# Attention with forget gates: the gates' sums ride in the second score product, under the low halves of the keys

## The chip, the cores and the metric

The kernel runs on one core of a Trainium2 chip. The metric is the device time of one execution in microseconds. Three runs of the kernel before took 1725.48, 1726.19 and 1727.21 us; the median is 1726.19 us.

## The reference

Two transformer blocks on 512 tokens. The change lies in the second block, in its eight attention heads with forget gates ("forget heads" below, `fox` in the code):

```python
def _fox_attention(q, k, v, log_f):
    """softmax(q.k/sqrt(d) + c[t] - c[s]) over s <= t, c = cumsum(log f)."""
    scale = HEAD_DIM ** -0.5            # HEAD_DIM = 64, 8 heads
    c = jnp.cumsum(log_f.astype(jnp.float32), axis=-1)
...
        logits = jnp.einsum('bhqd,bhkd->bhqk', qi, k, preferred_element_type=jnp.float32) * scale
        logits = logits + ci[..., None] - c[:, :, None, :]
        logits = jnp.where(kpos[None, :] <= qpos[:, None], logits, -jnp.inf)
        p = jax.nn.softmax(logits, axis=-1)
        return jnp.einsum('bhqk,bhkd->bhqd', p.astype(v.dtype), v)
```

The term `c[t]` is the same for all keys of a query and drops out of the softmax. What the kernel needs is `-q.k*scale + c[s]`, the score with its sign turned, and the kernel's softmax works on that.

## The kernel before

Everything lies transposed in SBUF: 128 partitions (features) by 512 tokens. float32 accuracy comes from splitting: each operand `x` is kept as a high part `xh` (rounded to the matmul's format, fp32r) and a low part `xl = x - xh`; `hi_lo` and `pair` (L120 to L150) do this, the high part by a cast on ScalarE (L136), the low part by a subtraction on VectorE (L140). A linear layer takes three matmuls for each block of 128 features (`mm3`, L208 to L210): high by high, high by low, low by high. These three lines are the bulk of the kernel. Weights are loaded by SP in pieces of 128 by 1024 into a ring of three raw tiles `wr` (`wload`, L180), then split into `wh` and `wl`.

A forget head has only 64 features, half of the 128 rows that TensorE reduces over, and the kernel fills both halves. `place` (L850) copies 64 rows of one tile into the upper or lower half of another, by a DMA of 128 KB on SP's queue. For a head, `stacked` makes one tile `stk` with the queries' high part above and their low part below; `doubled` makes two tiles `dbl`: the keys' high part twice, and the keys' low part twice. One matmul of the first pair then gives `qh.kh + ql.kh`, one of the second `qh.kl + ql.kl`. That takes six copies a head. `fox_inputs` (L1286) does it for a pair of heads; from pair 1 on it first computes the pair's queries and keys with two linear layers.

The gates' sums `c` come from a small matmul over the normed input (16 matmuls of 40 by 512, L1177), then on VectorE and ScalarE an addition, a scale, a bias, log-sigmoid (`Abs`, `Exp`, `Ln`), and a cumulative scan (L1189). They are kept in `cf`, whose other rows are zero: the high part of head `hd` in row `hd` (L1192, ScalarE), the low part in row `32 + hd` (L1193, VectorE).

`fox_scores` (L1263) runs over four blocks of 128 queries. Block `i` sees `w = 128, 256, 384 or 512` keys and has three matmuls into one PSUM bank: the two above (L1269, L1270) and a third (L1271), in which column `hd` of the constant `sel_r` picks rows `hd` and `32 + hd` of `cf` and adds their sum to every query's row. Then `softmax`: VectorE reads the bank, adds the mask and finds the minimum (L814), ScalarE takes the exponential with its sum (L171), VectorE the reciprocal (L817), ScalarE scales (L821). The scores use three banks in turn (`AT`, banks 70, 71, 72). `fox_values` transposes the weights of the attention on TensorE (L828), splits them, and multiplies by the values (L1210, L1211).

Between the heads stand independent products: the queries and keys of later heads and of the next kind of head (`sb_raw`), and `memory` (L945), which loads four `mem` tiles, squares them for a norm on ScalarE (L349), and splits them (`mh` on ScalarE, L138; `ml` on VectorE, L142).

The order of instructions on each engine is not that of the code. The tile framework's scheduler sets it (`TileContext(schedule_with_timeline_sim=True)`, L1694), from its own costs; at run time every engine, and SP's queue of DMAs, then runs in that order. SBUF tiles come from a list of 84 slots, given out in the order in which they were freed (`A`, `free`).

Of the kernel before, what the change touches and what calls it, by code (L numbers as in the profile page):

```python
# [11 lines left out]
F32R = mybir.dt.float32r  # L12
# [5 lines left out]
P = 128  # L18
T = 512
# [19 lines left out]
for _n, _w in _VECS:  # L39
# [4 lines left out]

_CONSTS = [
    ("ident", 128), ("later", 128), ("incl", 128), ("strict", 128), ("nstrict", 128),
    ("ones", 128), ("chunk", 14), ("sel", 8), ("invf", 1), ("sgn", 1),
    ("mchunk", 512), ("mcausal", 512),
]
COFF = {}  # L50
# [8 lines left out]
def two_blocks(ctx: ExitStack, tc: tile.TileContext, d, dbg=None):  # L59
    nc = tc.nc  # L60
    V, S, G, PE = nc.vector, nc.scalar, nc.gpsimd, nc.tensor
# [14 lines left out]
    def A(name, dt=F32, cols=T):  # L76
        if cols > 256 or len(spare_half) < 3:
            i = spare.popleft()
            low[0] = min(low[0], len(spare))
            ap = ar.tile([P, T], dt, tag="slot%d" % i, name=name)[:, :cols]  # L80
            owner[id(ap)] = (spare, i, ap, name)
        else:
            i = spare_half.popleft()
            ap = ar.tile([P, 256], dt, tag="half%d" % i, name=name)[:, :cols]
            owner[id(ap)] = (spare_half, i, ap, name)
        return ap

    def free(*xs):
        for x in xs:
            if isinstance(x, (tuple, list)):  # L90
                free(*x)
            else:
                home, i = owner.pop(id(x))[:2]
                home.append(i)
# [118 lines left out]
    def lin(w, n, hs, cols=T, k0=0, after=None):  # L213

        kt = len(hs)
        ps = MM()
        wt = wtile(w, n, kt, k0)
        for k in range(kt):
            r = mm3(ps[:, :cols], wpart(wt, k), hs[k], k == 0, k == kt - 1)
            if k == 0 and after:  # L220
                order(r, after)
        free(wt[1])
        return ps
# [202 lines left out]
    def C(name):  # L426
        i = COFF[name]
        return con[:, i:i + dict(_CONSTS)[name]]
# [9 lines left out]
    def const_r(name):  # L438
        c = C(name)
        o = cst.tile([P, c.shape[1]], F32R, name=name + "_r")  # L440
        V.tensor_copy(o, c)
        return o

    later_r, incl_r, ones_r = const_r("later"), const_r("incl"), const_r("ones")
    ident_r, nstrict_r, sel_r = const_r("ident"), const_r("nstrict"), const_r("sel")
    chunk_r = const_r("chunk")

    def normed(src_tiles, gain, n, before=None, **kw):
# [11 lines left out]
    def evac(ps, name, Rt, scale=None, cols=T):  # L460
        o = A(name)
        if scale is None:
            V.tensor_tensor(o[:, :cols], ps[:, :cols], Rt[:, :cols], ALU.mult)
        else:
            V.scalar_tensor_tensor(o[:, :cols], ps[:, :cols], scale, Rt[:, :cols], ALU.mult, ALU.mult)
        return o
# [76 lines left out]
    def chained(src, gain, n, step=None):  # L543

        hs = [(A("hh", F32R), A("hl", F32R)) for _ in src]
        st = Stat(n, esq=S, eadd=G)
        for c in HALVES:
            steps, los = [], []
            for k, x in enumerate(src):
                steps.append(step(k, c) if step else [])  # L550
                hold[:] = hi_lo(hs[k][0][:, c], hs[k][1][:, c], x[:, c], vcol(gain, k))
                los.append(hold[1])
                st.add(x[:, c], c)
            if step:

                line = []
                for k in range(KD + 2):
                    line += steps[k] if k < KD else []
                    line += [los[k - 2]] if k > 1 else []
                for later, earlier in zip(line[1:], line):  # L560
                    order(later, earlier)
        return hs, st
# [60 lines left out]
    hs, pss, wps, marks = [], [MM(), MM()], [], []  # L623
    for k, x in enumerate(xs):
        hs.append(pair("h", x, vcol("pre_mix", k)))
        marks.append(list(made))
        if k in (0, 2, 4):
            c = PARTS[k // 2]
# [11 lines left out]
    R, rt = st.done()  # L640
# [13 lines left out]
    for t in range(NT):  # L654
        q = slice(t * P, (t + 1) * P)
        ps = AT()
# [153 lines left out]
    def softmax(ps, w, mask):  # L810

        s, p = A("sc", F32, w), A("p", F32, w)
        mn, su = small(1), small(1)
        V.tensor_tensor_reduce(s[:, :w], ps[:, :w], mask, 1.0, BIG, ALU.add, ALU.min, mn)  # L814
        act(table_exp[0], p[:, :w], s[:, :w], AF.Exp, bias=mn, scale=-1.0, accum_out=su)
        free(s)
        V.reciprocal(su, su)  # L817
        if table_exp[0] == "exp_tanh":
            V.tensor_scalar(p[:, :w], p[:, :w], su, None, ALU.mult)
        else:  # L820
            S.activation(p[:, :w], p[:, :w], AF.Copy, scale=su)  # L821
        return p
# [25 lines left out]
    def place(o, rows, src, a):  # L848

        nc.sync.dma_start(f(o[rows]), f(src[a]))  # L850

    HALF = (slice(0, 64), slice(64, 128))

    def stacked(p, hh):

        o = A("stk", F32R)
        for rows, src in zip(HALF, p):
            place(o, rows, src, HALF[hh])
        return o
# [104 lines left out]
    for n in range(KD):  # L964
        g = gbs[n]
        ps = lin(d["w_o_mla"], n, oms)
# [6 lines left out]
    def post_norm(fs, st, gain, xs):  # L973

        def step(k, c):
            r = V.scalar_tensor_tensor(fs[k][:, c], fs[k][:, c], vcol(gain, k), st.R[:, c], ALU.mult, ALU.mult)  # L976
            q = (G if k % 2 else V).tensor_tensor(xs[k][:, c], xs[k][:, c], fs[k][:, c], ALU.add)
            if c.stop == T:
                free(fs[k])
                if k == KD - 1:  # L980
                    free(st.R)
            return [r.ins] if k % 2 else [r.ins, q.ins]
        return step
# [23 lines left out]
    hs, sth = chained(xs, "pre_ffn", DM, post_norm(fs, st, "post_mix", xs))  # L1007
# [12 lines left out]
    R = sth.R  # L1020
# [57 lines left out]
    for n in range(G1, KF, 2):  # L1078
# [4 lines left out]
        else:  # L1083
            for j, g in enumerate(zg):
                act("silu", g, g, AF.Silu)
                ps = lin(d["w_fgu"], 2 * (n + j) + 1, ns)
                V.tensor_tensor(g, g, ps, ALU.mult)
                hid.append(repair(g))
        if n + 2 == G2:
            for m in range(KD):  # L1090
                ps = lin(d["w_fd"], m, hid, k0=G1)
# [24 lines left out]
    hs, sth = chained(xs, "attn_norm", DM, post_norm(fs, st, "post_ffn", xs))  # L1116
# [45 lines left out]
    R = sth.R  # L1162
# [11 lines left out]
    ps = MM()  # L1174
    for k in range(KD):
        for part in range(2):
            PE.matmul(ps[0:40], lhsT=wfr[:, 40 * k:40 * k + 40], rhs=hs[k][part],  # L1177
                      start=k + part == 0, stop=k + part == KD)
# [11 lines left out]
    cf = A("cf", F32R)  # L1190
# [2 lines left out]
    V.tensor_tensor(cf[32:40], ef[0:8], f(cf[0:8]), ALU.subtract)  # L1193
    free(zf, ef)

    def doubled(p, hh):

        out = []
        for src in p:
            o = A("dbl", F32R)  # L1200
            for rows in HALF:
                place(o, rows, src, HALF[hh])
            out.append(o)
        return out
# [55 lines left out]
        free(ah, al)  # L1260
        return r

    def fox_scores(hd, qst, k2):  # L1263
        pt = []
        for i in range(NT):
            w = (i + 1) * P
            q = slice(i * P, (i + 1) * P)
            ps = AT()
            PE.matmul(ps[:, :w], lhsT=qst[:, q], rhs=k2[0][:, :w], start=True, stop=False)  # L1269
            PE.matmul(ps[:, :w], lhsT=qst[:, q], rhs=k2[1][:, :w], start=False, stop=False)  # L1270
            PE.matmul(ps[:, :w], lhsT=sel_r[:, hd:hd + 1].broadcast_to([P, P]), rhs=cf[:, :w],  # L1271
                      start=False, stop=True)
            pt.append(softmax(ps, w, C("mcausal")[:, T - w:]))
        free(qst, k2)
        return pt

    def fox_values(hd, pt, o):
# [8 lines left out]
    def fox_inputs(hp):  # L1286
        if hp:
            xq = evac(lin(d["w2T"], hp, hs), "fq", R, -0.125)
            xk = evac(lin(d["w2T"], 4 + hp, hs), "fk", R)
        else:  # L1290
            xq, xk = firsts[0], firsts[4]
        pq, pk = repair(xq), repair(xk)
        out = [(stacked(pq, hh), doubled(pk, hh)) for hh in range(2)]
        free(pq, pk)
        return out

# [33 lines left out]
    for hd in range(8):  # L1330
# [12 lines left out]
        else:  # L1343
            sraw.append(sb_raw(hd // 2))
        last = (hd, pt, o)
    free(hs, R)
    share(mm=(0, 1, 2), at=(3, 4, 5, 6), op=(7,))
    sin_ = [sb_inputs(*sraw[0])]
    fox_values(*last)
# [62 lines left out]
    hs, sth = chained(xs, "xattn", DM)  # L1412
# [8 lines left out]
    R = sth.R  # L1421
# [45 lines left out]
    q1 = [repair(q, eh=G) for q in firstq[4:]]  # L1467
# [19 lines left out]
    hs, sth = chained(xs, "ffn_norm", DM)  # L1487
# [5 lines left out]
    R = sth.R  # L1493
# [115 lines left out]
def _constants():  # L1609
    i = np.arange(P)  # L1610
    a, b = i[:, None], i[None, :]
    c = {}
    c["ident"] = a == b
    c["later"] = (a // 64 == b // 64) & (a > b)
    c["incl"] = a >= b
    c["strict"] = b > a
    c["nstrict"] = np.where(b > a, 0.0, -BIG)
    c["ones"] = np.ones((P, P))
    c["chunk"] = a // 64 + 6 == np.arange(14)[None, :]
    c["sel"] = (a < 64) & (a % 32 == np.arange(8)[None, :])  # L1620
    c["invf"] = np.array(_INVF, np.float32)[i % 32][:, None]
    c["sgn"] = np.where(a % 64 < 32, -1.0, 1.0)
    z = np.zeros((P, T - P))
    c["mchunk"] = np.concatenate([z, np.where(b // 64 <= a // 64, 0.0, BIG)], 1)
    c["mcausal"] = np.concatenate([z, np.where(b <= a, 0.0, BIG)], 1)
    return np.concatenate([np.asarray(c[n], np.float32) for n, _ in _CONSTS], 1)
# [72 lines left out]
```

## Time and profile before

| what | value |
|---|---|
| median of three runs | 1726.19 us |
| the profiled execution | 1726.83 us |
| its span, first to last instruction | 1725.1 us |
| TensorE busy, 930 to 1060 us (scores of the forget heads) | 128.69 of 130 us |
| third products (L1271) | 32, from 955.7 to 1057.6 us |

The profile is of one execution. In its rows a matmul's duration overlaps the next one's; how far apart two starts are says what a matmul costs while TensorE is never idle. "Idle before" in a row is the time in which an engine waited, with the instruction that ended the wait. DMA rows of SP show when a transfer was issued; "to landing" is from there to the end of the transfer.

### The profile page before, as it was taken

The numbers are of one execution on the slowest core, as the hardware profiler recorded it, in microseconds if no ns is written. First come the engines' busy times: TensorE is split into PE (matmuls) and PEld (weight loads), VectorE is DVE, ScalarE is ACT, GpSimd is POOL, SyncE is SP. The second block draws the span as 40 slices with busy tenths as digits, with TensorE's granted clock in tenths as the row PEclk, the third lists the DMA queues.
The fourth block names the chain that finished last, engine by engine and source line by source line (L and its number), as shares of the span: only waits on it lengthen the run. The fifth ranks groups of instructions, "written<-read, shape, count | busy, mean of one in ns | idle before, by whom it ended". The sixth has DMA issues, their size and how long they took to land.

```text
span 1725.1 us, 25847 instructions
## 1 busy us (share of the span) xinstructions
PE 1700.7 (99%) x9706; PEld 1485.8 (86%) x9706; DVE 1197.4 (69%) x2390; ACT 886.9 (51%) x1821; POOL 92.0 (5%) x109
## 2 busy tenths in 40 slices
PE   9999999999999999999999999999999999999998
PEld 7888888888888889989998888898898988988987
DVE  7547764677666767747777656877866598865863
ACT  6534454555454444424445656778535454552553
POOL 1000001000004000000013000000200200000000
PEclk9999999999999999999999999999999999999999
DMA  6212152223540322332333353442314123232321
GB/s 228 86 49 74 63 171 86 79 80 97 193 168 1 108 86 77 123 110 74 124 110 100 97 134 102 131 135 83 126 51 133 50 71 106 95 120 74 108 88 50
DMA packets 63951, 174.30 MB, mean 101 GB/s; under 512 B 8081, under 2 KB 13393, under 8 KB 63825
## 3 DMA queue, kind: packets, MB, share of 16 engines
q1 hardware_dynamic: 63408, 172.44, 32.3%
q8 instruction: 76, 1.25, 0.3%
q14 instruction: 51, 0.41, 0.1%
q10 hardware_dynamic: 288, 0.14, 0.0%
q0 software_dynamic: 128, 0.07, 0.0%
HBM read 153.74 MB, written 4.19 MB: 92 GB/s over the span
## 4 chain that ended last, share of the span: by engine, by line
PE 88%; DVE 4%; DMA 3%; ACT 2%; issue 1%; POOL 0%; POOLq 0%; DVEq 0%; SPq 0%; ACTq 0%
PE bank L208 27%; PE bank L210 27%; PE bank L209 27%; DVE wl L140 1%; PE bank L828 1%; PE bank L1251 1%; ACT wh L136 1%; DVE f L976 1%; DMA wr<-w_mq 0%; DMA wr<-w1K 0%; PE bank L1211 0%; DVE hl L142 0%; PE bank L1210 0%; DMA wr<-w1T 0%; PE bank L376 0%
## 5 line engine op out<-in xcount | busy, mean ns | idle before, releaser
L136 ACT CAST wh<-wr 128x512 fp32r<-128x512 f32 (+2 forms) x534 | 311.7, 606 | 356.9 <-PE bank L209 129.8
L140 DVE TENSOR_TENSOR wl<-wr,wh 128x512 fp32r<-128x512 f32 (+1 forms) x534 | 349.4, 671 | 162.4 <-ACT wh L136 137.7
L210 PE MATMUL bank<-hh,wl 128*128 128x512 f32 (+1 forms) x868 | 305.1, 353 | 0.8 <-DVE wl L140 0.8
L208 PE MATMUL bank<-hh,wh 128*128 128x512 f32 (+1 forms) x868 | 303.4, 355 | 2.2 <-DVE z L1016 1.7
L209 PE MATMUL bank<-hl,wh 128*128 128x512 f32 (+1 forms) x868 | 304.6, 352 | 0.7 <-DVE hl L142 0.6
L209 PE MATMUL bank<-prl,wh 128*128 128x256 f32 (+1 forms) x760 | 253.5, 334 | 0.0
L210 PE MATMUL bank<-prh,wl 128*128 128x256 f32 (+1 forms) x760 | 253.0, 334 | 0.0
L208 PE MATMUL bank<-prh,wh 128*128 128x256 f32 (+1 forms) x760 | 250.9, 334 | 0.2 <-ACT wh L136 0.2
L210 PEld LDWEIGHTS bank<-hh,wl 128*128 128x128 f32 x868 | 164.3, 189 | 23.0 <-DVE wl L140 2.1
L208 PEld LDWEIGHTS bank<-hh,wh 128*128 128x128 f32 x868 | 163.3, 190 | 23.7 <-ACT hh L138 3.4
L209 PEld LDWEIGHTS bank<-hl,wh 128*128 128x128 f32 x868 | 164.4, 189 | 22.0 <-DVE hl L142 2.0
L208 PEld LDWEIGHTS bank<-prh,wh 128*128 128x128 f32 x760 | 144.3, 190 | 14.1 <-ACT wh L136 0.4
L209 PEld LDWEIGHTS bank<-prl,wh 128*128 128x128 f32 x760 | 144.4, 190 | 13.8
L210 PEld LDWEIGHTS bank<-prh,wl 128*128 128x128 f32 x760 | 144.3, 190 | 13.8
L209 PE MATMUL bank<-nl,wh 128*128 128x512 f32 (+1 forms) x440 | 148.4, 337 | 0.0
L208 PE MATMUL bank<-nh,wh 128*128 128x512 f32 (+1 forms) x440 | 148.3, 337 | 0.0
L210 PE MATMUL bank<-nh,wl 128*128 128x512 f32 (+1 forms) x440 | 147.9, 337 | 0.0
L209 PEld LDWEIGHTS bank<-nl,wh 128*128 128x128 f32 x440 | 83.5, 190 | 8.9
L210 PEld LDWEIGHTS bank<-nh,wl 128*128 128x128 f32 x440 | 83.5, 190 | 8.9
L208 PEld LDWEIGHTS bank<-nh,wh 128*128 128x128 f32 x440 | 83.5, 190 | 8.8
L333 POOL TENSOR_TENSOR rtok<-sm,minus_half 128x2 f32<-128x2 f32 (+1 forms) x20 | 17.2, 859 | 1194.1 <-DVE sm L332 1194.1
L136 ACT CAST wh<-s 128x512 fp32r<-128x512 f32 x72 | 43.9, 620 | 65.0 <-DVE s L297 37.9
(400 smaller groups left out, 3354.4 us busy)
## 6 DMA issues: line engine op xcount, KB each, us to landing
wr<-w_up SPq DMA_DIRECT2D x38, 512.0 KB, 3.5
wr<-w_fgu SPq DMA_DIRECT2D x32, 512.0 KB, 3.6
wr<-w1T SPq DMA_DIRECT2D x16, 512.0 KB, 3.5
wr<-w_gate SPq DMA_DIRECT2D x16, 512.0 KB, 4.3
wr<-w_fd SPq DMA_DIRECT2D x16, 512.0 KB, 4.0
wr<-w2T SPq DMA_DIRECT2D x16, 512.0 KB, 4.0
wr<-w_dn SPq DMA_DIRECT2D x16, 512.0 KB, 3.5
wr<-w1K SPq DMA_DIRECT2D x12, 512.0 KB, 4.2
```

The costliest lines, as they stand in the source:

```text
L136: r = S.copy(hi, src) if eh is S else V.tensor_copy(hi, src)
L140: q = el.tensor_tensor(lo, src, f(hi), ALU.subtract)
L208: r = PE.matmul(ps, lhsT=ah, rhs=bh, start=first, stop=False)
L209: PE.matmul(ps, lhsT=ah, rhs=bl, start=False, stop=False)
L210: PE.matmul(ps, lhsT=al, rhs=bh, start=False, stop=last)
L333: G.tensor_tensor(y, v, minus_half[:, :y.shape[1]], ALU.pow)
L828: PE.transpose(tp[:, i * P:(i + 1) * P], ps_tiles[i][:, b * P:(b + 1) * P], C("ident"))
L976: r = V.scalar_tensor_tensor(fs[k][:, c], fs[k][:, c], vcol(gain, k), st.R[:, c], ALU.mult, ALU.mult)
L1251: PE.matmul(z[:, (b2 - b) * P:w], lhsT=lt, rhs=part[:, :T - b2 * P], start=False, stop=False)
```

## The change

The third product of a score goes. Its two rows of sums enter by the second product. Head `hd` now has four tiles: `qst` (queries' high part above the low part, as before), `k0` (keys' high part twice, as before), `q1` (queries' high part above, the lower half of `pick` below), and `k1` (keys' low part above, 64 rows of `cf` from row `hd` below, so that the head's sums lie in rows 64 and 96). `pick` is a new tile of 512 equal columns, one in rows 64 and 96 and zero elsewhere. The second matmul gives `qh.kl + c`; the product `ql.kl` is no longer computed. A head takes eight copies in place of six, two of them from `pick` and `cf`.

```diff
-    ("ones", 128), ("chunk", 14), ("sel", 8), ("invf", 1), ("sgn", 1),
+    ("ones", 128), ("chunk", 14), ("sel", 1), ("invf", 1), ("sgn", 1),
...
-    ident_r, nstrict_r, sel_r = const_r("ident"), const_r("nstrict"), const_r("sel")
+    ident_r, nstrict_r = const_r("ident"), const_r("nstrict")
...
+    pick = A("pick", F32R)
+    V.tensor_copy(pick, C("sel").broadcast_to([P, T]))
...
-    def fox_scores(hd, qst, k2):
+    def fox_scores(hd, qst, q1, k0, k1):
...
-            PE.matmul(ps[:, :w], lhsT=qst[:, q], rhs=k2[0][:, :w], start=True, stop=False)
-            PE.matmul(ps[:, :w], lhsT=qst[:, q], rhs=k2[1][:, :w], start=False, stop=False)
-            PE.matmul(ps[:, :w], lhsT=sel_r[:, hd:hd + 1].broadcast_to([P, P]), rhs=cf[:, :w],
-                      start=False, stop=True)
+            PE.matmul(ps[:, :w], lhsT=qst[:, q], rhs=k0[:, :w], start=True, stop=False)
+            PE.matmul(ps[:, :w], lhsT=q1[:, q], rhs=k1[:, :w], start=False, stop=True)
             pt.append(softmax(ps, w, C("mcausal")[:, T - w:]))
-        free(qst, k2)
+        free(qst, q1, k0, k1)
...
-        out = [(stacked(pq, hh), doubled(pk, hh)) for hh in range(2)]
+        out = []
+        for hh in range(2):
+
+            k0, q1, k1 = A("dbl", F32R), A("stk", F32R), A("dbl", F32R)
+            hd, h = 2 * hp + hh, HALF[hh]
+            qst = stacked(pq, hh)
+            for rows in HALF:
+                place(k0, rows, pk[0], h)
+            place(q1, HALF[0], pq[0], h)
+            place(q1, HALF[1], pick, HALF[1])
+            place(k1, HALF[0], pk[1], h)
+            place(k1, HALF[1], cf, slice(hd, hd + 64))
+            out.append((qst, q1, k0, k1))
...
-    free(hs, R)
+    free(hs, R, pick)
...
-    c["sel"] = (a < 64) & (a % 32 == np.arange(8)[None, :])
+    c["sel"] = (a == 64) | (a == 96)
```

The scheduler then sets another order. Three places show it. In the new file the two products of a score are L1272 and L1273.

The first place is VectorE in the norm ahead of the forget heads, where `f`, `x`, `sq` and `hl` are steps of that norm and `wfr` holds the gates' weights. Before:

```order
L1031 TENSOR_TENSOR f<-f,bank_69 128x256
L1171 TENSOR_SCALAR wfr<-con 128x320
L977 TENSOR_TENSOR x<-x,f 128x256
L976 SCALAR_TENSOR_TENSOR f<-f,vec,R 128x256 x2
L362 TENSOR_TENSOR sq<-sq 128x256
L1172 CAST wfr<-wf 128x8x8
```

Now, on the same engine at the same place:

```order
L1031 TENSOR_TENSOR f<-f,bank_69 128x256
L1171 TENSOR_SCALAR wfr<-con 128x320
L977 TENSOR_TENSOR x<-x,f 128x256
L976 SCALAR_TENSOR_TENSOR f<-f,vec,R 128x256 x2
L1197 CAST pick<-con 128x512
L362 TENSOR_TENSOR sq<-sq 128x256
L1172 CAST wfr<-wf 128x8x8
```

The cast that makes `pick` was put among the steps of the norm.

The second place is TensorE where head 0's first three scores get their last product; banks 66 and 69 collect products of linear layers. Before:

```order
L208 MATMUL bank_66<-hh,wh 128x512
L1271 MATMUL bank_70<-cf,sel_r 128x128
L1271 MATMUL bank_71<-cf,sel_r 128x256
L1271 MATMUL bank_72<-cf,sel_r 128x384
L209 MATMUL bank_66<-hl,wh 128x512
```

Now:

```order
L210 MATMUL bank_69<-hh,wl 128x512
L1273 MATMUL bank_70<-dbl,stk 128x128
L1273 MATMUL bank_71<-dbl,stk 128x256
L1273 MATMUL bank_72<-dbl,stk 128x384
L1272 MATMUL bank_70<-dbl,stk 128x512
L1273 MATMUL bank_70<-dbl,stk 128x512
L1272 MATMUL bank_72<-dbl,stk 128x256
L1273 MATMUL bank_72<-dbl,stk 128x256
L210 MATMUL bank_66<-hh,wl 128x512
```

The last product comes eight linear products earlier, and the next two scores, which before stood 14 linear products later, follow at once.

The third place is SP's queue and ScalarE just behind the sums. SP before, from the last weight load ahead of pair 1's copies on (`wr` of `w2T` are weights of coming linear layers):

```order
L180 DMA wr_75<-w2T 128x1024
L180 DMA wr_76<-w2T 128x1024
L850 DMA dbl<-prh 64x512 x2
L850 DMA dbl<-prl 64x512 x2
L850 DMA dbl<-prh 64x512 x2
L850 DMA dbl<-prl 64x512 x2
L180 DMA wr_74<-w2T 128x1024
```

SP now:

```order
L180 DMA wr_75<-w2T 128x1024
L850 DMA dbl<-prh 64x512 x3
L850 DMA dbl<-prl 64x512
L850 DMA dbl<-cf 64x512 x3
L850 DMA dbl<-prh 64x512
L850 DMA dbl<-prl 64x512
L850 DMA dbl<-cf 64x512
L950 DMA mem<-memT 128x512
L180 DMA wr_76<-w2T 128x1024
L180 DMA wr_74<-w2T 128x1024
```

ScalarE now, a little later (`p` and `sc` are the softmax's tiles):

```order
L349 ACTIVATE sq<-mem 128x256
L138 ACTIVATE mh<-mem,vec 128x256
L349 ACTIVATE sq<-mem 128x256
L138 ACTIVATE mh<-mem,vec 128x256
L171 ACTIVATE p,sm_101<-sc,sm_100 128x512
L821 ACTIVATE p<-p,sm_97 128x256
L171 ACTIVATE p,sm_106<-sc,sm_105 128x256
L136 CAST wh<-wr_76 128x512
```

The last `mem` load and a weight load that stood ahead of the sums on SP stand behind four copies of them, and on ScalarE the passes over that `mem` tile stand ahead of softmax pieces and of the cast of that weight.

## The prediction

> **What bounds the kernel now.** The first view is the page: busy time of each engine, and the chain that ended last.
>
> ```profile
> PE 1700.7 (99%) x9706; PEld 1485.8 (86%) x9706; DVE 1197.4 (69%) x2390; ACT 886.9 (51%) x1821; POOL 92.0 (5%) x109
> PE 88%; DVE 4%; DMA 3%; ACT 2%; issue 1%; POOL 0%; POOLq 0%; DVEq 0%; SPq 0%; ACTq 0%
> ```
>
> TensorE holds 88% of the chain. The second view is by stretches (busy time of PE, PEld, DVE, ACT, POOL, then the granted clock): 930 to 1060 us holds the forget heads' scores, 1060 to 1330 us the stage after them.
>
> ```profile
> 930.00:1060.00 130.00, 128.69 (x645) 106.11 (x644) 82.47 (x212) 81.78 (x198) 0.69 (x1) 1.00 0.43 112
> 1060.00:1330.00 270.00, 264.25 (x1666) 236.23 (x1665) 205.32 (x432) 171.25 (x388) 16.33 (x20) 1.00 0.38 111
> ```
>
> TensorE idles 130 - 128.69 = 1.3 us in the stage that is changed, and the clock is full. So a matmul that goes saves what it spaces out in the issue order, and a new wait of TensorE costs its whole length: there is nothing that it could hide in.
>
> **What is removed.** The third view is TensorE's timeline at the removed matmuls (start, duration, operation).
>
> ```profile
> 943.47 0.40 PE L209 MATMUL bank<-hl,wh 128*128 128x512 f32 x1
> ...
> 955.49 0.39 PE L208 MATMUL bank<-hh,wh 128*128 128x512 f32 x1
> 955.72 0.57 PE L1271 MATMUL bank<-cf,sel_r 128*128 128x128 f32 x3
> 956.12 0.40 PE L209 MATMUL bank<-hl,wh 128*128 128x512 f32 x1
> ...
> 959.78 0.40 PE L1271 MATMUL bank<-cf,sel_r 128*128 128x512 f32 x1
> 960.02 0.28 PE L1269 MATMUL bank<-dbl,stk 128*128 128x256 f32 x1
> ```
>
> Durations overlap, so I take starts. Three third products, of 128, 256 and 384 columns, hold TensorE from 955.72 to 956.12, 0.40 us; the one of 512 from 959.78 to 960.02, 0.24 us. That is 0.64 us a head; 8 heads give **5.1 us**. The first two products stay, with other operands in the same shapes.
>
> The Trainium skill ("TensorE: Matmul & The Clock Gate", Back-to-back issue gap) states a spacing of N/2.4 ns plus 2.5 ns for warm matmuls. By it a head's four would be 543 ns and the eight heads 4.3 us, an estimate from that page, and the whole change 0.8 us worse. The rows are longer at 512 columns (0.24 us where it gives 0.216) and for the three together (0.40 against 0.327), so the trace's 5.1 us stands.
>
> **What is added.** A head needs eight half-tile copies on SP's queue instead of six, 16 more in all.
>
> ```profile
> 935.07 1.11 SPq L850 DMA_DIRECT2D stk<-prh  x2
> 936.28 1.19 SPq L850 DMA_DIRECT2D stk<-prl  x2
> ```
> ```profile
> DMA to landing us min/median/max: 2.2/2.4/2.9
> ```
>
> Two copies take 1.2 us of SP, 0.6 us each, and land 2.4 us after issue (the second fence is of the `dbl` copies). 16 x 0.6 = 9.6 us, of 130 us in which SP mostly waits. I cost that at nothing where copies run ahead, with TensorE's long blocks of other products as cover; without that cover every late microsecond shows.
>
> VectorE makes `pick`, and the order puts this in the norm ahead of the stage, where TensorE waits at the end of a chain through VectorE and GpSimd:
>
> ```profile
> 907.97 0.43 PE L384 MATMUL bank<-con,rtok 128*128 128x128 f32 x2 [0.99 <-POOL rtok L333]
> ```
> ```profile
> L136 DVE CAST prh<-mq 128x512 fp32r<-128x512 f32 x6 | 2.6, 425 | 0.2
> ```
>
> No row shows a cast from one broadcast column. The nearest is the plain 512-column cast, 0.43 us; the passes of 0.69 us below are the far end, and nothing is the near end, if another step of the chain is late. I take **0.5 us** more of that wait.
>
> **What is moved: when the gates' sums are needed.** Before, the sums `cf` entered last, by a matmul that read them directly. Now they are finished, then copied by DMA, before the second product.
>
> ```profile
> 938.03 0.40 PE L208 MATMUL bank<-hh,wh 128*128 128x512 f32 x1
> ```
> ```profile
> 938.43 3.71 PE bank L1177 x16
> ```
> ```profile
> 948.21 0.69 DVE L463 TENSOR_TENSOR fk<-bank,R 128x512 f32<-128x512 f32 x1 [0.29 <-PE bank L210]
> ...
> 951.24 0.68 DVE L1193 TENSOR_TENSOR cf<-ef,cf 8x512 fp32r<-8x512 f32 x1
> ```
>
> `cf` is ready at 951.92 and its first reader starts at 955.72: 3.8 us of slack. In the new order the 16 gate matmuls stand two rows later (0.46 us), but the product of `fk`, which VectorE evacuates ahead of the scan, ends 0.4 us earlier; I get the same 952.0. The first copy of `cf` goes out at 952.05 and lands at **954.5** (954.3 to 955.0). TensorE comes to the second products earlier now: from 938.03, 3 products, the gate matmuls, 3 products, 0.40 us of first scores, then 44 products of 0.227 us (53 spacings from 943.47 to 955.49): 938.03 + 0.69 + 3.72 + 0.68 + 0.40 + 9.98 = **953.5**. So a new wait of 1.0 us (0.8 to 1.5); behind it stand products whose operands are ready, and they wait too.
>
> Right behind, TensorE waits for VectorE to empty the score banks, since the 14 products that filled that time stand elsewhere now.
>
> ```profile
> 955.98 0.29 DVE L814 CUSTOM_DVE_ANT_0 sc<-bank,con 128x128 f32<-128x128 f32 x1 [1.26 <-PE bank L1271]
> ...
> 957.01 0.08 DVE L814 DVE_READ_ACCUMULATOR2_ANT sm<- 128x1 f32 x1
> ```
>
> VectorE starts 0.26 us after the first score and needs 1.1 us for three (955.98 to 957.09). Two scores that reuse these banks stand in that time, then a product whose low weights VectorE makes only after it: about 0.85 us of waits.
>
> **The next late thing** is ScalarE. The last `mem` load now stands behind four copies of `cf` on SP, and four ScalarE passes over it stand ahead of a softmax piece, then of the cast of a weight.
>
> ```profile
> L349 ACT ACTIVATE sq<-mem x8: 400/408/426, 923.4 to 950.6; 128x256 f32<-128x256 f32 x8
> L138 ACT ACTIVATE mh<-mem,vec x8: 493/496/507, 923.7 to 957.2; 128x256 fp32r<-128x256 f32 x8
> ...
> DMA to landing us min/median/max: 2.6/3.4/4.0
> ```
> ```profile
> 960.95 0.72 ACT L171 ACTIVATE p<-sc,sm 128x512 f32<-128x512 f32 x1 [1.46 <-DVE sm L814]
> 961.58 0.19 ACT L171 ACTIVATION_READ_ACCUMULATOR p<-sc,sm 128x1 f32 x1
> 961.67 0.49 ACT L171 ACTIVATE p<-sc,sm 128x256 f32<-128x256 f32 x1
> 962.08 0.19 ACT L171 ACTIVATION_READ_ACCUMULATOR p<-sc,sm 128x1 f32 x1
> 962.17 1.10 ACT L821 ACTIVATE p<-p,sm 128x512 f32<-128x512 f32 x2
> ...
> 966.20 0.62 ACT L136 CAST wh<-wr 128x512 fp32r<-128x512 f32 x1 [0.17 <-PE bank L1211]
> ```
>
> Six copies behind 952.05 put the load at 955.75; it lands at 959.15 (958.4 to 959.8). Four passes (1.8 us, 1.45 as they overlap by 0.1 each), the exponentials of 512 and 256 columns (0.72 and 0.50 by their starts), a scaling (0.4) and the cast (0.62) end at **962.9** (962.1 to 963.5). TensorE's own work from 953.5 to that weight's product is 22 products of 0.227, the scores and small ones, 6.4 us: 959.9. So the three waits together are 3.0 us, fixed by this last; the two earlier alone give 1.85.
>
> In exchange two waits of before in this stretch can go.
>
> ```profile
> PE bank L1269 <- DVE sm L814: 0.4, 1, 0.4
> PE bank L376 <- DVE sm L814: 0.4, 1, 0.4
> ```
>
> With TensorE's restart they are 0.45 us apiece, 0.9 us. Given back: 3.0 - 0.9 = 2.1 us, or 1.0 if the load is early. I take 1.9, near the median landings.
>
> **The sum.** 5.1 - 0.5 - 1.9 = 2.7 us less. From the profiled execution's 1726.83 (span 1725.1 and 1.7 around it) that is 1724.1; it lies 0.64 above the median 1726.19, so on the median **1723.5**, 0.16% less. The orders differ on to 1330 us, which I can't cost row by row: the 5.75 us of idle there bound a gain; I take nothing, and 1.5 us either way.
>
> **Rivals.**
>
> *The whole gain arrives.* `cf`'s copy or the `mem` load comes early, and the two old waits go: 5.1 less, 1721.1 (1719.6 to 1722). For it: 3.8 us of slack today. Against: 952.0 plus 2.4 is later than 953.5 by any row.
>
> *The gain is eaten.* Loads at their late ends (4.0 and 2.9 us) add 1 us, the later heads or the next stage 2: about 1726, no change. For it: SP carries added copies and weights in one line. Against: from head 2 on a score comes well after its copies.
>
> *Slower: SP starves TensorE of weights.* The four `cf` copies wait for VectorE, and the next four weight loads stand behind them on SP. Each microsecond that `cf` is later than 952.0 delays these loads, casts and products one for one. It decides against the change once the extra waits pass 5.1 + 3.5 = 8.6 us, so with `cf` 6 us late or a second such block at heads 4 to 7: 1730 and more. Against: `cf`'s chain has fixed steps. The Trainium skill ("TensorE: Matmul & The Clock Gate", Part 1: The HAM clock gate) says that an idle window of about 3.4 us halves TensorE's clock, which would add to such a block; no row here shows it.
>
> That the third product doesn't really go is excluded by the order: no row of it is left.
>
> **How the numbers follow.** About 0.2% (3.5 us) is what a measurement can tell from no change, so the border is 1722.7, inside the forecast's own spread (1721.8 to 1725.3). Forecast 0.52, whole gain 0.24, eaten 0.16, slower 0.08. Faster: 0.24 and a quarter of the forecast, 0.37; slower 0.08; same 0.55. Range: the whole gain with 1.5 us of luck after it, 1719.6; the eaten case and 1.3 more, 1727.3. Beyond lie the slower case and thin tails.
>
> **What would show it.** Right: no third product; a wait for a `dbl` copy near 953.5 of 1 us, one for a cast of ScalarE near 962 with `mem` ahead of it; the wait for `rtok` near 908 at 1.5 us; idle time from 930 to 1060 of 3.2 us instead of 1.3. Wrong: no wait at the first second product (`cf` or its copy was earlier), or over 2 us at a later head's score or weight.

## The result and the profile after

The changed kernel takes **1750.6 us** (median of 4 runs, 1749.0 to 1751.3) beside 1726.6 us before (1725.5 to 1727.2). The ratio is 1.0140, with a 95% interval of 1.0128 to 1.0152: 24 us slower. The forecast was 1723.5 us, in a range up to 1727.3.

The first line of the page of the changed kernel, and its chain that ended last:

```profile
PE 1705.3 (98%) x9674; PEld 1484.4 (85%) x9674; DVE 1196.6 (68%) x2390; ACT 884.3 (51%) x1821; POOL 93.3 (5%) x109
PE 85%; DVE 5%; DMA 3%; ACT 3%; issue 2%; POOL 0%; SPq 0%; POOLq 0%; DVEq 0%; ACTq 0%
```

The span grew from 1725.1 to 1747.2 us, by 22.1. TensorE has 32 matmuls less and is busy 4.6 us longer (1705.3 against 1700.7); the other 17.5 us are idle time (41.9 against 24.4). Both are strange, and the view by stretches says where they are (PE busy, the clock, DMA share, GB/s; below it the same rows of before):

```profile
930.00:1060.00 130.00, 119.42 (x555) 0.97 0.47 128
1060.00:1330.00 270.00, 255.64 (x1596) 0.99 0.35 102
1330.00:1700.00 370.00, 370.00 (x2114) 1.00 0.30 93
```
```profile
930.00:1060.00 130.00, 128.69 (x645) 1.00 0.43 112
1060.00:1330.00 270.00, 264.25 (x1666) 1.00 0.38 111
1330.00:1700.00 370.00, 370.00 (x2125) 1.00 0.27 86
```

From 930 to 1330 us TensorE idles 24.9 us where it idled 7.1; all of the new idle time lies there. It isn't one wait. The waits of TensorE from 930 to 1060 us, after (line, what ended the wait: total, times, longest):

```profile
PE bank L1213 <- ACT pth L136: 2.2, 2, 1.6
PE bank L1272 <- DVE ptl L140: 2.0, 3, 0.8
PE bank L210 <- DVE wl L140: 1.9, 3, 1.4
PE bank L208 <- ACT wh L136: 1.5, 2, 1.1
PE bank L828 <- DVE sm L814: 1.4, 3, 0.8
```

Casts of weights (`wh`, `wl`), pieces of the softmax (`sm`), and splits of its transposed result (`pth`, `ptl`): every supplier of TensorE is late now and then, the longest by 0.8 to 1.6 us. No row names a copy of the gates' sums. The second loss is the clock. TensorE's timeline near 1026 us (in brackets the idle time before):

```profile
1022.97 0.50 PE L1213 MATMUL bank<-pth,v 128*128 128x512 f32 x1 [1.56 <-ACT pth L136]
...
1026.20 0.80 PE L210 MATMUL bank<-hh,wl 128*128 128x512 f32 x1 [1.42 <-DVE wl L140]
1026.79 0.63 PE L208 MATMUL bank<-hh,wh 128*128 128x512 f32 x1
1027.22 0.63 PE L209 MATMUL bank<-hl,wh 128*128 128x512 f32 x1
...
1032.74 0.40 PE L208 MATMUL bank<-hh,wh 128*128 128x512 f32 x1
1032.98 0.39 PE L209 MATMUL bank<-hl,wh 128*128 128x512 f32 x1
```

Two products of 512 columns stand 0.43 us apart up to about 1032 us and 0.23 to 0.24 us from there: the granted clock was halved. By the same view this happens near 1217 and 1248 us too, for 3.4 us each; 13.6 us at half clock lose 6.8 us of work. Less the 5.1 us of matmuls that are gone, that is 1.7 us; the other 2.9 of the 4.6 us aren't located (a matmul behind a wait shows 0.50 us where one takes 0.40, which may be part of it).

One row of SP's queue hints at a place further back (waits of SP, 930 to 1070 us, after and before):

```profile
SPq L850 <- PE bank L828: 21.3, 2, 12.9
```
```profile
SPq L850 <- PE bank L828: 6.3, 3, 3.7
```

The longer of the two waits, 12.9 us, is that of a copy of `pick` for head 4 (TensorE's row that it waited for, then SP's timeline, the copy and the first load of weights behind it):

```profile
983.56 0.33 PE L1272 MATMUL bank<-dbl,stk 128*128 128x256 f32 x1
```
```profile
983.92 0.47 SPq L850 DMA_DIRECT2D stk<-pick  x1
...
989.56 0.60 SPq L180 DMA_DIRECT2D wr<-w2T  x1
```

The view names a transpose (L828), which starts just behind this product; by the program the copy's tile held keys of head 2 before, and a first product of its scores (L1272) is their last reader. So a tile was asked for while it was in use, and the load of weights stood behind on the queue. This shows that such waits exist, not what they cost: SP had waits as long before (13.0 us, of a load of weights), and from 984 to 1000 us TensorE waited only 0.2 us for a weight.

### The profile page after: what moved, and what is told of

Its sections match the earlier page's. It is cut to its first block, busy times and chain, and to the rows that moved or that the text cites. A ratio compares the mean times of both kernels' runs of the same rounds, so it can differ in the third digit from the quotient of the medians.

```text
span 1747.2 us, 25785 instructions
## 1 busy us (share of the span) xinstructions
PE 1705.3 (98%) x9674; PEld 1484.4 (85%) x9674; DVE 1196.6 (68%) x2390; ACT 884.3 (51%) x1821; POOL 93.3 (5%) x109
## 4 chain that ended last, share of the span: by engine, by line
PE 85%; DVE 5%; DMA 3%; ACT 3%; issue 2%; POOL 0%; SPq 0%; POOLq 0%; DVEq 0%; ACTq 0%
PE bank L208 27%; PE bank L210 27%; PE bank L209 27%; DVE wl L140 1%; DMA wr<-w_o_mla 1%; ACT wh L136 1%; DVE f L976 1%; PE bank L1254 1%; DMA wr<-w_mq 1%; PE bank L828 1%; DMA wr<-w1K 0%; DMA wr<-w_out 0%; DVE sq L362 0%; DVE hl L142 0%; PE bank L376 0%
## 5 line engine op out<-in xcount | busy, mean ns | idle before, releaser
L333 POOL TENSOR_TENSOR rtok<-sm,minus_half 128x2 f32<-128x2 f32 (+1 forms) x20 | 17.5, 875 | 1214.6 <-DVE sm L332 1214.6
```

The lines of the kernel that those rows point to most:

```text
L333: G.tensor_tensor(y, v, minus_half[:, :y.shape[1]], ALU.pow)
```

## The experiments

Each time stands beside runs of the kernel before on the same chip, whose median lay between 1725.9 and 1726.4 us. Behind a time stands its ratio to them, with the 95% interval. The theories, as they came up:

- **SP**: the added copies on SP hold back loads of weights.
- **Cover**: with fewer matmuls TensorE reaches the softmax too early.
- **Order**: any edit makes the scheduler give another order, with more waits.
- **Tiles**: too few tiles are free, and a tile's next use waits for its last reader.
- **Handing out**: tiles are enough, but they are handed out in turn, and so the wrong ones.

### The third products alone

The kernel before without them (so its scores leave the gates' sums out), in the scheduler's order:

```diff
-            PE.matmul(ps[:, :w], lhsT=qst[:, q], rhs=k2[1][:, :w], start=False, stop=False)
-            PE.matmul(ps[:, :w], lhsT=sel_r[:, hd:hd + 1].broadcast_to([P, P]), rhs=cf[:, :w],
-                      start=False, stop=True)
+            PE.matmul(ps[:, :w], lhsT=qst[:, q], rhs=k2[1][:, :w], start=False, stop=True)
```

> The kernel before with the third product of the scores left out and nothing in its place: the gates' sums are not added, and six copies a head stay. Three theories for the 24 us. SP: the copies of pick and cf, which wait on SP for freed tiles or for the sums, hold the weight loads behind them; then this kernel is about 5 us faster than before, 1721. Cover: with 5.1 us fewer matmuls TensorE outruns the softmax on VectorE and ScalarE; then it is slow too, 1740 or more. Order: any change of instructions makes the scheduler give another order with more waits, whatever its content; then it lies anywhere between 1721 and 1750, and not near 1721 by rule.

Measured: 1733.7 us, ratio 1.0044 (1.0027 to 1.0061). Less work and nothing else in the code, and it is slower. SP and its copies can't be the whole of it.

Then the same, with every engine held to the order of the kernel before, less the 32 matmuls. This is done at the end of the program, by a table of instruction numbers for each engine; `order` fixes who is issued first and waits for nothing:

```diff
+    plan = {}
+    for ins in nc.all_instructions():
+        plan.setdefault(str(ins.engine).split(".")[1], []).append(ins)
+    for eng, rows in PLAN.items():
+        seq = [plan[eng][a + j] for a, n in zip(rows[::2], rows[1::2]) for j in range(n)]
+        for a, b in zip(seq, seq[1:]):
+            order(b, a)
     return low[0]
```

> The kernel before without the 32 third products, as in the run without them, but now every engine is held to the order of the kernel before, with only those 32 matmuls taken out of TensorE's (the scores leave the gates' sums out). Order (what costs time is that any edit makes the scheduler give another order, with more short waits): 1721 us, 5 us less than before, against 1733.7 for the same work in the scheduler's own order. Cover (with fewer matmuls TensorE reaches the softmax too early, whatever the order): still 1728 or more. Tiles (scarce tiles force waits): 1721 too, since here as many tiles are free as before.

Measured: 1723.5 us, 0.9988 (0.9979 to 0.9998). The order alone is worth 10 us between these two runs. The matmuls are worth 2.4 us (0.3 to 3.6), not 5.1: TensorE's idle time from 930 to 1330 us is 9.4 us (before 7.1), so it gives some 2.3 us back in waits, and Cover holds to that extent. The profiled execution is the slowest of ten (1726.6 us), but it lost its time ahead of this stage: from the start of the last gate product (L1177) to that of the first product with `moh`, the input of a later linear layer, it takes 350.9 us, and before 353.6.

### The third products put back

The changed kernel, with a third product that adds zero (a zero column of a constant against `cf`):

```diff
-            PE.matmul(ps[:, :w], lhsT=q1[:, q], rhs=k1[:, :w], start=False, stop=True)
+            PE.matmul(ps[:, :w], lhsT=q1[:, q], rhs=k1[:, :w], start=False, stop=False)
+            PE.matmul(ps[:, :w], lhsT=chunk_r[:, 0:1].broadcast_to([P, P]), rhs=cf[:, :w],
+                      start=False, stop=True)
```

> The changed kernel with a third product put back that adds zeros (a zero column of a constant against cf), so TensorE has the 32 matmuls again and all new copies stay. SP: the waits stay and 5 us of matmuls come on top or fill some of them, 1748 to 1755. Cover: the waits go, 1732 or less. Order: anything from 1726 to 1755.

Measured: 1743.9 us, 1.0106 (1.0088 to 1.0124): 32 matmuls more, and 7 us faster than the changed kernel, again in another order. The number of matmuls isn't what decides.

### No copies of `pick`

Four fixed `q1` tiles, whose lower halves GpSimd fills once:

```diff
-    pick = A("pick", F32R)
-    V.tensor_copy(pick, C("sel").broadcast_to([P, T]))
+    q1s = [A("stk", F32R) for _ in range(4)]
+    for q1 in q1s:
+        G.tensor_scalar(q1[64:128], C("sel")[64:128].broadcast_to([64, T]), 1.0, 0.0, ALU.mult, ALU.add)
...
-            place(q1, HALF[1], pick, HALF[1])
```

> The changed kernel, but with four q1 tiles kept through the stage, their lower halves written once by GpSimd; the copies of pick on SP go (seven copies a head instead of eight), and nothing on SP waits for a q1 tile of the list of slots. SP: the two waits of 13 and 8 us of SP for a tile's last reader go, and 10 us or more of the 24 come back: 1740 or less. Cover: no better than 1748. Order: anything.

Measured: 1745.1 us, 1.0111 (1.0096 to 1.0126). With eight copies less on SP some 5 us of 24 come back, half of what SP was to give; order and tiles differ here too, so not even these 5 us are surely SP's.

### Tiles held, work unchanged

The kernel before computes what it did, but five tiles (or two) are taken from the list through the forget heads:

```diff
     free(zf, ef)
+    held = [A("held") for _ in range(5)]
...
-    free(hs, R)
+    free(hs, R, held)
```

> The kernel before, with five SBUF tiles held and not used through the stage of the forget heads, as many as the change keeps more of at a time (four q1 and pick); the computation is that of before. SP by its copies alone, and cover: no change, 1725 to 1728. If it is the scarcer tiles, with every tile reused sooner, that make the waits: 1740 or more. Order: moves by more than 2 us either way.

> The kernel before with the same work, and two tiles held through the heads with forget gates, which leaves at the least eight free where ten were, as in the changed kernel (with five held it was 1748). Tiles: between the two, about 1732 to 1740, with waits on a tile's last reader on SP. Order: anything from 1730 to 1750, not in step with the number held. Cover: 1726.

Measured: five held, **1748.1 us**, 1.0126 (1.0109 to 1.0143); two held, 1731.1 us, 1.0033 (1.0020 to 1.0046). Nothing of the change is in these kernels, and five missing tiles cost nearly what the change does. The bare number of free tiles doesn't settle it, though: at its scarcest the changed kernel has eight free, as the kernel with two held. With five held the waits are of the same kind as in the changed kernel (stretches, then waits):

```profile
930.00:1060.00 130.00, 118.33 (x559) 0.96 0.41 112
1060.00:1330.00 270.00, 262.50 (x1630) 0.99 0.36 106
```
```profile
PE bank L828 <- DVE sm L814: 2.7, 2, 1.6
PE bank L210 <- DVE wl L140: 2.2, 2, 1.2
PE bank L1211 <- ACT pth L136: 1.9, 2, 1.5
```

In the first stretch it idles as the changed kernel does (11.7 and 10.6 us), in the second less (7.5 and 14.4). Its busy time by the page is 1710.2 us, 9.5 above before's, so the clock takes its share here too.

### Another order with all tiles

The list of free tiles turned by five, or a head's tiles built in another sequence; work and number of tiles as before:

```diff
     free(zf, ef)
+    spare.rotate(-5)
```
```diff
-        out = [(stacked(pq, hh), doubled(pk, hh)) for hh in range(2)]
+        out = [(doubled(pk, hh), stacked(pq, hh))[::-1] for hh in range(2)]
```

> The kernel before with the same work and as many tiles; only the list of free tiles is turned by five ahead of the heads with forget gates, so that other tiles are handed out and the scheduler gives another order. Order: 1735 to 1750 us, as with five tiles held. Tiles: 1726 within 3 us, since none is scarcer. Cover: 1726.

> The kernel before with the same work and as many tiles; only the two tiles of doubled keys of a head are built ahead of its stacked queries instead of behind them. Order: 1730 to 1750 us. Tiles: 1726 within 3 us. Cover: 1726.

Measured: 1730.1 us, 1.0024 (1.0014 to 1.0033), and 1730.4 us, 1.0020 (1.0010 to 1.0029). So the order of the kernel before is a good one among several, and an edit that says nothing costs 4 us. That leaves some 20 us of the changed kernel's loss, or 14 by the 10 us that the scheduler's order cost without the third products.

### The order of before, with the tiles that are left

Why not simply keep the order? For each kernel one can count, from the program, the requests that stand in the order of the kernel before ahead of the last reader of the tile that they get: none in the kernel before, 11 in the one with the list turned, 36 with two tiles held, 64 with five, 52 in the changed kernel. Most ask tiles for casts of weights. (In the kernel with a head's tiles built in another sequence there is none either, and it lost 4 us: the count isn't the whole of it.) In these runs the order is kept, and such an instruction moves back just behind what it needs.

> The kernel before with five tiles held (1748 us in the scheduler's own order), now held on every engine to the order of the kernel before, as far as the tiles allow: where a tile's next use would come ahead of its last reader, the instruction moves back just behind what it needs (53 casts of weights, the matmuls on those weights and a few copies). Order: 1726 to 1731 us. Tiles (the scarce tiles make the waits, whatever the order): 1740 or more, with the same waits for casts of weights.

> The changed kernel (1750.6 us in the scheduler's own order), every instruction that both kernels have held to the order of the kernel before in the same way; the second products stand at the third ones' places, the copies of the gates' sums on SP at the places of the dropped copies of keys. Order: 1722 to 1728 us, the two or three us that the smaller count of matmuls is worth, less a wait of one or two us for the first copies. Tiles: 1740 or more. SP (its copies hold the weights): 1735 or more, with ScalarE's casts waiting for weight loads.

> The version with four fixed tiles for the second stationary operand, whose lower halves GpSimd fills once (1745 us in the scheduler's own order), held to the order of the kernel before in the same way; SP has one copy less a head. Order: 1722 to 1727 us. Tiles: 1738 or more. SP: 1730 or less, below the run with the copies of the pick tile.

Measured: **1814.4 us**, 1.0509 (1.0493 to 1.0525); **1808.6 us**, 1.0484 (1.0466 to 1.0501); 1824.9 us, 1.0570 (1.0554 to 1.0585). All three expectations of Order were far off. Waits of TensorE from 930 to 1060 us with five held:

```profile
PE bank L208 <- ACT wh L136: 18.8, 10, 4.7
```

The row fits weights that can't be cast ahead, since their tiles are still in use. With tiles handed out like this the old order isn't to be had, and the scheduler's own, at 1748 to 1751 us, is far better than the old one patched.

### Which tile is handed out

The tile of each request comes from a table. It is chosen so that, in the order of the kernel before, the tile's last reader is past, and of such tiles mostly the one given back last:

```diff
+    fit, fit_half = deque(SLOT_OF), deque(HALF_OF)
...
-            i = spare.popleft()
+            i = fit.popleft()
+            spare.remove(i)
```

First the kernel before with five tiles held. Not one request is early now, and every engine runs the order of the kernel before exactly:

> The kernel before with five tiles held, as in the run of 1748 us; but which free tile each request gets is read from a table, chosen so that in the order of the kernel before no tile is asked for ahead of its last reader. With it every engine runs the order of the kernel before exactly. Handing out (the number of tiles is enough, but free tiles are handed out in the order in which they were given back in the program's text, and with fewer spare that asks for tiles still in use in the order that runs): 1726 us within 3. Tiles (five fewer are too few, whichever is handed out): 1740 or more.

Measured: **1731.4 us**, 1.0025 (1.0016 to 1.0034), from 1748. Being short of five tiles costs 5 us; the other 17 came from which tile was handed out and from the scheduler's order that came with it; this run doesn't part the two. (In the runs with a table, line numbers are three higher.)

```profile
930.00:1060.00 130.00, 125.87 (x623) 1.00 0.42 110
1060.00:1330.00 270.00, 263.44 (x1655) 1.00 0.38 112
```

The changed kernel with such a table and the order of before, the same table in the scheduler's order, and the copies of `cf` and `pick` on another queue (`nc.gpsimd.dma_start` in place of `place`):

> The changed kernel with such a table and the order of the kernel before (second products at the third ones' places, copies of the gates' sums at those of the dropped copies of keys; three tiles for copies of keys still come late). Handing out: 1722 to 1728 us, against 1750.6 for the changed kernel and 1808.6 with the same order and tiles handed out in turn. Tiles: 1740 or more. SP (its copies hold the weights): 1735 or more.

> The changed kernel with the same table, in the scheduler's own order. Handing out alone, without the order: 1728 to 1740 us. Tiles or SP: 1745 to 1755, as the changed kernel.

> The changed kernel with the table of tiles and the order of the kernel before (1743.5 us), where the copies of the gates' sums and of the pick tile go to GpSimd's DMA queue instead of SP's, so that SP has as many copies a head as before. SP: 1722 to 1730 us. If what remains is not SP's queue (late copies, fewer matmuls, tight tiles): 1738 or more. GpSimd's queue may be slower to start a copy; then the second products wait for it and the waits name these copies.

Measured: 1743.5 us, 1.0102 (1.0087 to 1.0117); 1746.9 us, 1.0119 (1.0101 to 1.0136); 1745.9 us, 1.0114 (1.0099 to 1.0129). These looked like a verdict for Tiles or SP, and weren't. The stretch from 1060 to 1100 us was the odd one, in the first of them:

```profile
1060.00:1100.00 40.00, 31.85 (x153) 0.87 0.44 107
```
```profile
PE bank L1234 <- DMA dbl<-prl: 2.1, 1, 2.1
PE bank L1233 <- DMA stk<-prl: 1.3, 1, 1.3
```

Waits for copies of the next stage's heads, which the change doesn't touch: my table had given eight of their copies the places of the dropped ones, some 1000 instructions early, so tiles were set aside for them too long. The two runs of the changed kernels in the section on the order of before carry the same mistake (the one with five tiles held, 1814 us, doesn't). Their 1808.6 and 1824.9 us are therefore not prices of the change, and whether a right table helps the scheduler's own order stays open. On GpSimd's queue a copy of `cf` landed 3.3 us after its issue, on SP's 2.4 us.

### Copies on SP alone

The kernel before, its order and tiles untouched, with two more copies a head behind those of the stacked queries:

```diff
+            for e in range(2):
+                nc.sync.dma_start(extra[4 * hp + 2 * hh + e], f(pq[e][HALF[hh]]))
```

> The kernel before, its work, tiles and order untouched, with two more copies of 128 KB a head on SP's queue (16 in all, of rows of the queries' high and low parts, to a place that nobody reads), right behind the copies of the stacked queries, as the changed kernel's second stationary operand has them. SP (each copy holds the queue for 0.6 us, and the weights' loads behind it have no slack): 1735 us or more, with ScalarE's casts waiting for weight loads. Cover and tiles: 1726 to 1729.

Measured: 1732.8 us, 1.0036 (1.0022 to 1.0051). So 16 copies that nobody reads cost 6.5 us in this order. ScalarE's casts wait for the weights behind them, and once for such a copy itself, which still read the tile that the cast writes (waits of ScalarE, 930 to 1100 us):

```profile
ACT wh L139 <- DMA wr<-w2T: 9.4, 3, 4.3
ACT wh L139 <- DMA extra<-prl: 3.7, 1, 3.7
```

Before, waits of the first kind were 2.6 us in two. Two reserves: these copies go to DRAM, not to tiles, and the profiled execution is the slowest of five (1739.2 us; the others took 1730.4 to 1734.8).

### The mistake mended, and the copies moved behind the weights

> The changed kernel with a table of tiles and the order of the kernel before, as in the run of 1743.5 us, with one mistake of that run's table taken out: it had given eight copies of the next heads' low keys (the stick-breaking ones) the places of the copies that the change drops, some 1000 instructions ahead of their own, so that eight tiles were set aside for them too long and their copies came late. Now no tile in this part is asked for ahead of its last reader. Tiles: the loss near 1060 to 1100 us goes (TensorE busy 39 of 40 us there, as before, where it was 31.9). SP (two copies more a head ahead of the weights): 1728 to 1733 us, the 6.5 us that 16 idle copies cost less the 2.4 us that the dropped matmuls are worth. If neither: 1740 or more.

> The same, with one difference on SP's queue alone: the copies for the second product (queries' high part, pick tile, low keys, gates' sums) are issued some 100 instructions of the whole program ahead of their first reader instead of right behind the others, so that loads of weights go ahead of them. SP: 1722 to 1727 us, below the run beside it by 3 us or more. If what remains is not SP's queue: the same as that run.

Measured: **1724.8 us**, 0.9993 (0.9983 to 1.0002), and **1721.4 us**, 0.9976 (0.9968 to 0.9985). The first runs the changed kernel's computation in the order of the kernel before, and is as fast as it; 26 us of the changed kernel's time were its order and the tiles behind it. The second differs in SP's order, and in its table of tiles, which was chosen anew for that; it is faster than the kernel before and the changed one, by 4.6 and 29 us. Stretches of the first, then of the second:

```profile
930.00:1060.00 130.00, 125.84 (x618) 1.00 0.49 128
1060.00:1100.00 40.00, 39.25 (x220) 1.00 0.61 153
1060.00:1330.00 270.00, 264.81 (x1672) 1.00 0.38 113
```
```profile
930.00:1060.00 130.00, 127.51 (x631) 1.00 0.51 131
1060.00:1330.00 270.00, 263.34 (x1661) 1.00 0.38 113
```

The clock is full again. What the last step surely takes away is one wait of the first, ahead of head 0's first scores (the wait, then SP's copies in the first and in the second):

```profile
943.42 0.64 PE L1275 MATMUL bank<-dbl,stk 128*128 128x128 f32 x3 [1.31 <-DMA dbl<-prh]
```
```profile
939.62 0.69 SPq L853 DMA_DIRECT2D stk<-pick  x1
940.41 1.20 SPq L853 DMA_DIRECT2D dbl<-prh  x2
```
```profile
936.40 1.83 SPq L853 DMA_DIRECT2D dbl<-prh  x3
```

Four copies of `q1` tiles stood ahead of that first copy of keys on SP, 0.6 us each; the last of them is shown. The wait is 1.3 of the 3.4 us between the two runs. From the start of the last gate product to that of the first product with `moh` it took 353.6 us before, 351.6 in the first run and 349.7 in the second; so the profiles place 1.8 of the 3.4 us in this stage, and most of the rest ahead of it. The last page's first line against before's (1700.7 busy of 1725.1):

```profile
PE 1694.7 (99%) x9674; PEld 1480.9 (86%) x9674; DVE 1193.8 (69%) x2390; ACT 873.8 (51%) x1821; POOL 93.0 (5%) x109
```

Of a span of 1719.8 us, 6.0 us are less busy and 0.7 us more idle. So the removed matmuls pay nearly in full, 4.6 us by the medians. In the stage itself 3.8 us arrive; the rest of the 5.3 us between the two spans lies mostly ahead of it, where no matmul was removed.

## Why the prediction was wrong, step by step

**The step that failed** is one sentence of the sum: "The orders differ on to 1330 us, which I can't cost row by row: the 5.75 us of idle there bound a gain; I take nothing, and 1.5 us either way." It measured 17.9 us of new idle time from 930 to 1330 us (9.3 us up to 1060, where the sum had 1.9, and 8.6 us behind, where it had nothing) and 6.8 us of lost clock, for which there was no term. The idle time of before does bound a gain, but it says nothing of a loss. What I left out is that one tile more for each head, and `pick`, change which free tile each later request gets. 52 requests then stand ahead of their tile's last reader in the old order, so it can't be kept, and the order that the scheduler gives has short waits everywhere. The runs show it by three steps: other tiles alone, work unchanged, bring the loss (1748.1 us); five tiles held and the old order exactly, 1731.4 us; the change itself with fitted tiles and the old order, 1724.8 us. So order and tiles together are the cause. How the 26 us divide between them isn't shown: an order alone cost 4 and 10 us where no request was early, and the changed kernel in the scheduler's own order with a right table was not run.

**5.1 us for the third products.** In the old order they gave 2.4 us (0.3 to 3.6), and in the last run the whole change gave 4.6 us (2.6 to 5.5). The spacing was read rightly; in the first case waits took half of it.

**0.5 us for `pick` in the norm chain.** The wait there went from 1.0 to 1.1 us (waits of TensorE from 890 to 930 us, before and after). The cast found room.

```profile
PE bank L384 <- POOL rtok L333: 1.0, 1, 1.0
PE bank L384 <- POOL rtok L333: 1.1, 1, 1.1
```

**Three waits of 3.0 us behind the sums.** The first copies of `cf` were issued at 951.67 us (worked out: 952.05), and the first second product started at 954.80 us, where the copy's landing was put at 954.5. But no wait stands there: waits for weights of 1.05 and 0.27 us came earlier, near 948 and 950 us, and covered it. (Without them TensorE would have come at 953.48; 953.5 was worked out.) The score banks cost 0.59 us at 955.95 us (worked out: 0.85), and the wait for a cast near 962 us didn't come.

```profile
948.15 0.50 PE L208 MATMUL bank<-hh,wh 128*128 128x512 f32 x1 [1.05 <-ACT wh L136]
949.68 0.50 PE L210 MATMUL bank<-hh,wl 128*128 128x512 f32 x1 [0.27 <-DVE wl L140]
...
954.80 0.57 PE L1273 MATMUL bank<-dbl,stk 128*128 128x128 f32 x3
955.95 0.49 PE L1272 MATMUL bank<-dbl,stk 128*128 128x512 f32 x1 [0.59 <-DVE sm L814]
```

**16 copies costed at nothing "where copies run ahead".** They cost 6.5 us as idle copies in the old order, and one wait of 1.3 us in the first of the last two runs. Their cover was TensorE's other products, but the weights of those products come by the same queue.

**The slower rival** had the right sign, at a chance of 0.08, and at most part of the mechanism: `cf` was on time, weights did come late behind copies, but the copies are the smaller part. Its point of decision, 8.6 us of extra waits, was passed by far. Its remark that no row showed a halved clock was true of the kernel before; three stretches after do.

## What to carry to other kernels

Where a scheduler sets the order and tiles come from a list, count before running how many requests of the changed kernel stand, in the old order, ahead of the last reader of the tile they get. None means that the old order can be kept, not that the scheduler will keep it (it didn't in two kernels here, which lost 4 and 10 us by that); 52 went with 24 us. And test a change with the order held: 1733.7 against 1723.5 us for the same work shows that the scheduler's next order can hide what the change itself is worth.

Copies that are free by their data aren't free by their queue: 16 that nobody reads cost 6.5 us here. Put those with time to spare behind the copies and loads that have none: the last run did so, lost a wait of 1.3 us by it, and is the fastest.

## What the runs showed of the hardware

**The clock halves without a long idle.** In the changed kernel no idle time ahead of the stretch at 1026 us is longer than 1.56 us (windows ahead of the stretches and in them: PE busy, then the clock):

```profile
1020.00:1026.00 6.00, 3.17 (x17) 0.95 0.43 105
1026.00:1033.00 7.00, 6.80 (x18) 0.56 0.62 158
1210.00:1217.00 7.00, 5.11 (x34) 0.97 0.13 40
1217.00:1221.00 4.00, 4.00 (x19) 0.63 0.25 66
1240.00:1247.00 7.00, 3.15 (x24) 1.00 0.51 184
1247.00:1252.00 5.00, 5.00 (x32) 0.66 0.33 105
```

Ahead of the first stretch TensorE was busy 3.17 of 6 us, in pieces, and then ran 6.8 us at half clock; ahead of the second it was busy even 5.11 of 7 us. Only the third has one long idle time ahead of it, 3.9 us. The Trainium skill ("TensorE: Matmul & The Clock Gate", Part 1: The HAM clock gate) puts the default half rate after an idle window of about 3.4 us, on a free-running window. The lengths seen here (6.8, 3.4 and 3.4 us) agree with that window; the idle time doesn't have to be whole. So a stage of short waits can cost more than their sum: the first two stretches alone lose 5.1 us on top of the idle time.

**Issuing a copy costs SP 0.6 us**, while it lands 2.4 us after issue (the eight copies of `cf` in the changed kernel: medians of 0.59 and 2.4 us); the next copy on the queue starts after the first of these times, not after the second.
